# Attention of a hybrid encoder: the order of scores, transposes and products with v in one run for each head pair

## The chip, the cores and the metric

The kernel runs on one core of a Trainium2 chip. The metric is device time in microseconds, from one execution of the whole program. Three runs of the kernel before took 1909.5, 1911.06 and 1911.25 us, a median of 1911.06. One more execution was taken with the hardware profiler, and the rows shown in this document come from it.

The engines are named as in the profile: PE is the matrix engine, PEld its loading of the stationary operand, DVE the vector engine, ACT the scalar engine, POOL the general engine, and SP the engine that issues most transfers.

## The reference

The program computes two layers of an encoder trunk over 512 tokens of 1024 channels, in float32. Each layer has a feed-forward block, a mixer and a second feed-forward block. The mixer is where the change lies:

```python
z = h @ w_in                       # q, k, v, uf, ga, gf
y_na = neighbourhood_attention(q, k, v, rpb) @ w_na_out
y_f = fourier_mix(uf) @ w_f_out
g_na, g_f = sigmoid(ga + gate_bias[0]), sigmoid(gf + gate_bias[1])
return (g_na * y_na + g_f * y_f) @ w_o
```

There are 8 heads of 64 channels. The tokens lie on a grid of 8 rows by 64 columns. A query sees 16 columns of keys around its own. The queries are cut into four blocks of 16 columns (128 queries), and each block reads a band of 32 columns (256 keys), adds a relative position bias and a mask, takes a softmax over the 256 keys and multiplies by v.

## The kernel before

**Numbers.** A float32 operand is split in two: a high part (written by ACT as a rounded copy) and a low part (written by DVE as the difference). A product is three matmuls, high x high, high x low and low x high (`mm3`, lines 292 to 294). Weights arrive as raw tiles and are split into `whi` (line 181) and `wlo` (line 184), two granules ahead of their use, with three buffers each. `split` (lines 298, 299, and 301, 302 with a factor) does the same to activations.

**Attention.** Two heads make a pair `hp` (0 to 3); its channels fill 128 partitions, head e in partitions 64e to 64e+63. A block of work `i` is half a pair: `i = 2 hp + pr`, and it holds two query blocks of both heads. For each block of work there are three parts:

- scores (`att_scores`, line 1123): 12 matmuls with 64 rows of contraction and 256 columns, the two heads in turn, each head in its own half of the rows and with its own bank of PSUM. Behind them comes the softmax: on DVE the sum with the bias and the maximum (line 1133) and the reciprocal (1142), on ACT the exponential (1139) and the scaling (1146). The result `s` is two tiles.
- transposes (`att_trans`, line 1155): 8 transposes of 128x128 into two banks, each then split into a `p` tile by ACT and DVE.
- product with v (`att_out`): 12 matmuls of 256 columns into one bank, whose result is split into the tile `o` of the pair, one head after the other.

`att_step(i)` runs, in this order, the product of block i-2, the transposes of block i-1 and the scores of block i. So a block's softmax has one step to finish. Between two steps stands other work for PE: a projection of q or k for a later pair (`proj_q`, `proj_k`, 24 matmuls of 512 columns in one bank, whose result DVE multiplies by R at line 977 before it is split), or rows of the product of the Fourier branch with its weights (`fill`, eight rows of 12 matmuls, copied by ACT at line 1210). `bias_for(hp)` loads the relative bias of a pair with four transfers on SP and adds the mask with six operations on POOL (line 1106); it has two pairs' worth of buffers.

**Order.** The text of the kernel gives an order. A planner in the build then fixes each engine's own queue: it goes by the order of the text and by when it reckons an operand to be ready, and it can put a later instruction first. Where a block of the text is marked as scheduled by hand, ACT and DVE keep the order of the text. Each engine then runs its queue strictly in order.

**Space.** PSUM is one pool of eight banks (`bank`), shared by all. A pool of 23 slots of 4 KB (`slot`, `hilo`) holds v and its shifted copies (7 tiles), q, k, o, p, the Fourier branch's y, the rows of its product (`fs`), the tiles t1 of the next stage and the raw weights of this stage. A smaller pool of the stage holds `s`, the bias and the mask; `swap_pools(0)` closes it, and with that the loads of the next stage's weights may begin.

Of the kernel before, what the change touches and what calls it, by code (L numbers as in the profile page):

```python
# [92 lines left out]
def encoder_kernel(  # L93
# [15 lines left out]
    def nm(s):  # L109
        uid[0] += 1  # L110
        return f"{s}_{uid[0]}"
# [4 lines left out]
    def hilo(s):  # L116
        t = slot(F32R, s, (2, T))
        return t[:, 0, :], t[:, 1, :]

    def bank(s="ps"):  # L120
        return pp.tile([P, T], F32, tag="ps", name=nm(s))
# [133 lines left out]
    class Stream:  # L255
# [26 lines left out]
        def next(self):  # L282
            self.prep(self.pos + 1 + AHEAD)
            it = self.items[self.pos]
            self.pos += 1
            return it.out
# [4 lines left out]
    def mm3(ps, lh, ll, rh, rl, start, stop, again=False):  # L291
        PE.matmul(ps, lh, rh, start=start, stop=False, skip_group_check=again)  # L292
        PE.matmul(ps, lh, rl, start=False, stop=False, skip_group_check=again)  # L293
        PE.matmul(ps, ll, rh, start=False, stop=stop, skip_group_check=again)  # L294
# [641 lines left out]
    def stage_mixer(l, norm, nxt):  # L936
        mp = mix_pool[0]

        def tmp(dt=F32, s="x"):
            return mp.tile([P, T], dt, tag="tmp", name=nm(s), bufs=8)  # L940
# [29 lines left out]
        def proj_T(scale):  # L970
            ps = bank()
            wh, wl = ws.next()
            for kt in range(DT):
                c = slice(kt * P, (kt + 1) * P)
                mm3(ps, wh[:, c], wl[:, c], *xs[kt], kt == 0, kt == DT - 1)
            t = tmp(s="q")
            V.tensor_tensor(t, ps, R, ALU.mult)
            hi, lo = hilo("q")
            split(hi, lo, t, scale)
            return hi, lo  # L980
# [104 lines left out]
        def proj_q(hp):  # L1085
            q[hp] = proj_T(DH**-0.5)

        def proj_k(hp):
            k[hp] = proj_T(None)
            o.append(hilo("o"))  # L1090

        def bias_for(hp):
            bms[hp] = []
            for e in range(2):
                res = mp.tile([P, 3, 256], F32, tag="bm", name=nm("bm"), bufs=4)
                b = mp.tile([P, BIAS_F], F32, tag="bw", name=nm("bw"), bufs=2)
                base = RPB_N - BIAS_F - ((l * NH + 2 * hp + e) * RPB_H + 7 * RPB_W + 15 - 16 + RPB_PAD)
                for i in range(2):
                    src = bass.AP(tensor=rpb.tensor, offset=base + 8 * i, ap=[[RPB_W, 8], [1, 8], [1, BIAS_F]])
                    nc.sync.dma_start(out=b[64 * i : 64 * i + 64, :], in_=src)  # L1100
                for c in range(3):
                    w = bass.AP(
                        tensor=b.tensor, offset=b.offset + BIAS_F - 1 - OFF[c],
                        ap=[list(b.ap[0]), [-8, 4], [-RPB_W, 8], [-1, 8]],
                    )
                    G.tensor_tensor(
                        res[:, c, :].rearrange("p (a b c) -> p a b c", a=4, b=8), w,
                        msk[:, c, :].rearrange("p (a b c) -> p a b c", a=4, b=8), ALU.add,
                    )
                bms[hp].append(res)  # L1110

        def att_scores(i):
            hp, pr = divmod(i, 2)
            (qh, ql), (kh, kl) = q[hp], k[hp]
            ps = [bank(), bank()]
            for jj in range(2):
                j = 2 * pr + jj
                ks = slice(BAND[j] * 64, BAND[j] * 64 + 256)
                qs = slice(j * P, (j + 1) * P)
                for i, (a, b) in enumerate(((qh, kh), (qh, kl), (ql, kh))):  # L1120
                    for e in range(2):
                        r = slice(64 * e, 64 * e + 64)
                        PE.matmul(
                            ps[e][:, jj * 256 : (jj + 1) * 256], a[r, qs], b[r, ks], start=i == 0, stop=i == 2
                        )
            s_ = [tmp(s="s"), tmp(s="s")]
            nmx = sp.tile([P, 4], F32, tag="nmx", name=nm("nmx"), bufs=4)
            sm = sp.tile([P, 4], F32, tag="sm", name=nm("sm"), bufs=4)
            rs = sp.tile([P, 4], F32, tag="rs", name=nm("rs"), bufs=4)
            for e in range(2):  # L1130
                for jj in range(2):
                    c, z = slice(jj * 256, (jj + 1) * 256), 2 * e + jj
                    V.tensor_tensor_reduce(
                        s_[e][:, c], ps[e][:, c], bms[hp][e][:, pr + jj, :], -1.0, -NEG, ALU.add, ALU.min, nmx[:, z : z + 1]
                    )
            for e in range(2):
                for jj in range(2):
                    c, z = slice(jj * 256, (jj + 1) * 256), 2 * e + jj
                    S.activation(
                        s_[e][:, c], s_[e][:, c], AF.Exp, scale=-1.0, bias=nmx[:, z : z + 1], accum_out=sm[:, z : z + 1]  # L1140
                    )
                V.reciprocal(rs[:, 2 * e : 2 * e + 2], sm[:, 2 * e : 2 * e + 2])
            for e in range(2):
                for jj in range(2):
                    c, z = slice(jj * 256, (jj + 1) * 256), 2 * e + jj
                    S.activation(s_[e][:, c], s_[e][:, c], AF.Copy, scale=rs[:, z : z + 1])
            return s_

        def att_trans(s_):
            res = []  # L1150
            for jj in range(2):
                pt = bank()
                for e in range(2):
                    for c in range(2):
                        PE.transpose(
                            pt[:, (2 * c + e) * P : (2 * c + e + 1) * P],
                            s_[e][:, jj * 256 + c * P : jj * 256 + (c + 1) * P], ident,
                        )
                hi, lo = hilo("p")
                split(hi, lo, pt)  # L1160
                res.append((hi, lo))
            return res

        def att_out(i, p_):
            hp, pr = divmod(i, 2)
            po = bank()
            hs = slice(hp * P, (hp + 1) * P)
            for jj in range(2):
                ph, pl = p_[jj]
                for c in range(2):  # L1170
                    vh, vl = vch[BAND[2 * pr + jj] + 2 * c]
                    cs = slice(c * 256, (c + 1) * 256)
                    mm3(po[:, jj * 256 : jj * 256 + 256], vh[:, hs], vl[:, hs], ph[:, cs], pl[:, cs], c == 0, c == 1)
            pv = po.rearrange("p (a e q) -> p a e q", a=2, e=2)
            oh, ol = [z[:, pr * 256 : pr * 256 + 256].rearrange("p (a q) -> p a q", a=2) for z in o[hp]]
            for e in range(2):
                r = slice(64 * e, 64 * e + 64)
                split(oh[r], ol[r], pv[r, :, e, :])

        sc, pt_ = {}, {}  # L1180

        def att_step(i):
            if 0 <= i - 2 < 8:
                att_out(i - 2, pt_.pop(i - 2))
            if 0 <= i - 1 < 8:
                pt_[i - 1] = att_trans(sc.pop(i - 1))
            if i < 8:
                sc[i] = att_scores(i)


        def rows_of(src, tb, w):
# [11 lines left out]
        def fill(src, to, i, w=None):  # L1203

            w = w or [ws.next(), ws.next()]
            for tb in range(TB):
                if tb % 2 == 0:
                    to[i, tb // 2] = slot(F32, "fs", (2, T))
                ps = rows_of(src, tb, w)
                S.activation(to[i, tb // 2][:, tb % 2, :], ps, AF.Copy)  # L1210
                yield
# [106 lines left out]
        for g in range(4):  # L1318
            four_ch(g)
        proj_q(1)  # L1320
        for hp in range(3):
            bias_for(hp + 1)
            att_step(2 * hp)
            proj_k(hp + 1)
            att_step(2 * hp + 1)
            if hp < 2:
                proj_q(hp + 2)

        def f_rows():
            for i in range(2):  # L1330
                yield from fill(yf, fs, i)


        B = {(i, j): [z[i].bitcast(F32)[:, :, j * 256 : (j + 1) * 256] for z in (hx, lx)] for i in range(2) for j in range(2)}
# [7 lines left out]
            V.tensor_tensor(t[0], t[0], t[1], ALU.add)  # L1342
            yield t

        f_fill = f_rows()
        for i in range(6, 8):
            next(f_fill)
            next(f_fill)
            att_step(i)
        next(f_fill)  # L1350
        next(f_fill)
        first = minus(B[0, 0], B[0, 1], "t1")
        next(first)
        att_step(8)
        swap_pools(0)
        next(f_fill)
        next(first)
        att_step(9)
        t12, _ = next(first)
        ws.prep(ws.pos + 2)  # L1360
        next(f_fill)
        bias = []
        for which in range(2):
            b_ = slot(F32, "gb", (D,))
# [278 lines left out]
```

## Time and profile before

| what | us |
|---|---|
| median of three runs | 1911.06 |
| the profiled execution | 1909.88 |
| its span, first to last instruction | 1908.1 |
| PE busy | 1894.6 (99%) |
| DVE busy | 1609.9 (84%) |
| ACT busy | 1162.8 (61%) |
| PE matmuls | 9189 instructions |
| attention, first score to last transpose, layer 1 | 405.90 to 476.30 |
| attention, first score to last transpose, layer 2 | 1352.30 to 1422.70 |

Times of a row are counted from the start of the span. A row of the timeline gives the start, the duration, the engine, the line, the operation, the tiles written and read, the shape of the array's part and of the operand, and a count of like instructions that followed at once; square brackets hold the idle time of the engine before it and what ended that. Matmuls are pipelined: one of 512 columns shows 0.39 us, but the next starts much earlier. So the pace of PE is read from the starts of rows, not from their durations.

### The profile page before, as it was taken

To read this page: it belongs to the slowest core of one execution; us is meant where nothing else is said; L and a number is where in the kernel's file an instruction comes from. 1 tells how busy PE (TensorE), PEld (TensorE's weight loads), DVE (VectorE), ACT (ScalarE), POOL (GpSimd) and SP (SyncE) were. 2 spreads that over 40 slices of the span, in tenths; PEclk is the share of its full clock that TensorE was granted. 3 is DMA by queue.
4 is the path that set the end of the run, shared out by engine and by line. 5 is a ranking of instruction groups with operands and counts; after the bars stand their busy time and mean duration, and the time that the engine had idled before them with its cause. 6 is when DMAs were issued, how large, how long until landed. Compare 5 with 4: busy or idle time off the path is not lost.

```text
span 1908.1 us, 25170 instructions
## 1 busy us (share of the span) xinstructions
PE 1894.6 (99%) x9189; PEld 1587.4 (83%) x9189; DVE 1609.9 (84%) x2000; ACT 1162.8 (61%) x1676; POOL 199.2 (10%) x246
## 2 busy tenths in 40 slices
PE   9999999999999999999999999999999999999998
PEld 7888888888888888888888888888888888888886
DVE  7877899586989987889997778995769899787898
ACT  6655665457666755566665556663675566555664
POOL 0101010300111010001010100103111101010010
PEclk9999999999999999999999999999999999999999
DMA  9776499321986777649877665974129867766594
GB/s 301 207 208 182 149 255 316 95 73 45 265 214 164 175 195 207 176 152 258 255 188 210 183 177 157 274 267 131 37 95 250 214 169 173 205 180 177 170 279 141
DMA packets 104924, 361.09 MB, mean 189 GB/s; under 512 B 12064, under 2 KB 14240, under 8 KB 104800
## 3 DMA queue, kind: packets, MB, share of 16 engines
q1 hardware_dynamic: 77856, 267.42, 39.9%
q0 software_dynamic: 26800, 92.04, 26.7%
q8 instruction: 72, 1.18, 0.2%
q14 instruction: 52, 0.43, 0.1%
q10 hardware_dynamic: 144, 0.02, 0.0%
HBM read 354.18 MB, written 2.11 MB: 187 GB/s over the span
## 4 chain that ended last, share of the span: by engine, by line
PE 98%; DVE 1%; DMA 1%; ACT 0%; issue 0%; DVEq 0%; ACTq 0%
PE A L453 9%; PE A L454 9%; PE A L456 9%; PE o L453 7%; PE o L454 7%; PE o L456 7%; PE ps L292 5%; PE ps L293 5%; PE ps L294 5%; PE B L453 5%; PE B L454 5%; PE B L456 5%; PE C L454 2%; PE C L453 2%; PE C L456 2%; PE tr L545 2%
## 5 line engine op out<-in xcount | busy, mean ns | idle before, releaser
L181 ACT ACTIVATE whi<-raw 128x1024 fp32r<-128x1024 f32 (+1 forms) x528 | 546.9, 1037 | 428.1 <-PE A L454 127.8
L184 DVE TENSOR_TENSOR wlo<-raw,whi 128x1024 fp32r<-128x1024 f32 (+1 forms) x528 | 629.0, 1196 | 195.7 <-ACT whi L181 194.3
L152 POOL DMA_DIRECT2D raw<-in_wst_dram x158 | 136.0, 870 | 1285.7 <-DMA raw<-in_wst_dram 574.5
L166 DVE TENSOR_TENSOR raw<-raw,raw 128x1024 f32<-128x1024 f32 (+1 forms) x146 | 172.2, 1189 | 1.2
L454 PE MATMUL A<-whi,xl 128*128 128x512 f32 x384 | 149.5, 389 | 0.0
L453 PE MATMUL A<-whi,xh 128*128 128x512 f32 x384 | 149.4, 389 | 0.0
L456 PE MATMUL A<-wlo,xh 128*128 128x512 f32 x384 | 110.5, 389 | 0.0
L176 ACT ACTIVATE whi<-raw 128x1024 fp32r<-128x1024 f32 (+1 forms) x79 | 81.8, 1035 | 41.5 <-PE A L454 12.5
L177 DVE SCALAR_TENSOR_TENSOR wlo<-raw,whi 128x1024 fp32r<-128x1024 f32 (+1 forms) x79 | 93.2, 1192 | 10.9 <-ACT whi L176 10.8
L638 ACT ACTIVATE th<-sn,rh 128x512 f32<-128x512 f32 x80 | 56.9, 714 | 69.0 <-DVE sn L527 69.0
L522 ACT ACTIVATE sn<-A 128x512 f32<-128x512 f32 x96 | 56.4, 589 | 49.4 <-PE A L456 49.4
L456 PEld LDWEIGHTS A<-wlo,xh 128*128 128x128 f32 x384 | 72.1, 188 | 15.0
L454 PEld LDWEIGHTS A<-whi,xl 128*128 128x128 f32 x384 | 72.1, 188 | 14.8
L453 PEld LDWEIGHTS A<-whi,xh 128*128 128x128 f32 x384 | 72.1, 188 | 14.8
L453 PE MATMUL B<-whi,t1h 128*128 128x512 f32 x192 | 76.2, 397 | 0.0
L453 PE MATMUL A<-whi,t3h 128*128 128x512 f32 x192 | 75.3, 392 | 0.0
L453 PE MATMUL C<-whi,xh 128*128 128x512 f32 x192 | 74.9, 390 | 0.0
L453 PE MATMUL A<-whi,t2h 128*128 128x512 f32 x192 | 74.9, 390 | 0.0
L454 PE MATMUL B<-whi,t1l 128*128 128x512 f32 x192 | 74.8, 390 | 0.0
L454 PE MATMUL A<-whi,t3l 128*128 128x512 f32 x192 | 74.8, 390 | 0.0
L454 PE MATMUL C<-whi,xl 128*128 128x512 f32 x192 | 74.7, 389 | 0.0
L454 PE MATMUL A<-whi,t2l 128*128 128x512 f32 x192 | 74.7, 389 | 0.0
(410 smaller groups left out, 4794.3 us busy)
## 6 DMA issues: line engine op xcount, KB each, us to landing
raw<-in_wst_dram SPq DMA_DIRECT2D x466, 512.0 KB
raw<-in_wst_dram POOLq DMA_DIRECT2D x162, 512.0 KB, 7.8
raw<-in_wst_dram SPq DMA_DIRECT2D x30, 256.0 KB
vs<-v SPq DMA_DIRECT2D x12, 256.0 KB
bw<-in_rpb_dram SPq DMA_DIRECT2D x32, 68.0 KB
x<-in_xin_dram SPq DMA_DIRECT2D x4, 512.0 KB
raw<-in_wst_dram POOLq DMA_DIRECT2D x8, 256.0 KB, 8.2
dft<-in_dft_dram POOLq DMA_DIRECT2D x8, 256.0 KB, 6.1
```

Source lines behind the costliest of these rows:

```text
L152: G.dma_start(out=self.t, in_=wst[GRAN_AT[self.plus]][:, 0 : self.n], accum_op=ALU.add)
L166: V.tensor_tensor(self.raw.t, self.raw.t, self.add.t, ALU.add)
L176: S.activation(hi, t, AF.Copy, scale=-1.0)
L177: self.last = V.scalar_tensor_tensor(lo, t, -1.0, hi.bitcast(F32), ALU.mult, ALU.subtract)
L181: S.activation(hi[:, cs], t[:, cs], AF.Copy)
L184: self.last = V.tensor_tensor(lo[:, cs], t[:, cs], hi[:, cs].bitcast(F32), ALU.subtract)
L292: PE.matmul(ps, lh, rh, start=start, stop=False, skip_group_check=again)
L293: PE.matmul(ps, lh, rl, start=False, stop=False, skip_group_check=again)
L294: PE.matmul(ps, ll, rh, start=False, stop=stop, skip_group_check=again)
L453: PE.matmul(ps, lh, rh, start=start, stop=False, skip_group_check=again)
L454: PE.matmul(ps, ll, rh, start=False, stop=False, skip_group_check=again)
L456: PE.matmul(ps, lh, rl, start=False, stop=stop, skip_group_check=again)
```

## The change

`att_scores` is cut in two: the matmuls stay under that name and return their banks, and the softmax becomes `att_probs`. `att_step` is replaced by two functions that work on a whole pair. `att_next(hp)` runs the transposes of both blocks of pair hp-1, then the scores of both blocks of pair hp, and then both softmaxes. `att_outs(hp)` runs the products with v of both blocks of pair hp. The bias of the next pair is now loaded after the scores, and the eight rows of the Fourier product are dealt out as 2, 2, 1, 2 and 1 where they were 2, 2, 2, 1 and 1.

```diff
         def att_scores(i):
...
+            return ps
+
+        def att_probs(i, ps):
+            hp, pr = divmod(i, 2)
             s_ = [tmp(s="s"), tmp(s="s")]
...
-        def att_step(i):
-            if 0 <= i - 2 < 8:
-                att_out(i - 2, pt_.pop(i - 2))
-            if 0 <= i - 1 < 8:
-                pt_[i - 1] = att_trans(sc.pop(i - 1))
-            if i < 8:
-                sc[i] = att_scores(i)
+        def att_outs(hp):
+            for i in (2 * hp, 2 * hp + 1):
+                att_out(i, pt_.pop(i))
+
+        def att_next(hp):
+            if hp:
+                for i in (2 * hp - 2, 2 * hp - 1):
+                    pt_[i] = att_trans(sc.pop(i))
+            if hp < 4:
+                ps = [att_scores(i) for i in (2 * hp, 2 * hp + 1)]
+                for i, p in zip((2 * hp, 2 * hp + 1), ps):
+                    sc[i] = att_probs(i, p)
...
-        for hp in range(3):
-            bias_for(hp + 1)
-            att_step(2 * hp)
-            proj_k(hp + 1)
-            att_step(2 * hp + 1)
-            if hp < 2:
-                proj_q(hp + 2)
+        for hp in range(3):
+            att_next(hp)
+            bias_for(hp + 1)
+            proj_k(hp + 1)
+            if hp:
+                att_outs(hp - 1)
+            if hp < 2:
+                proj_q(hp + 2)
+        f_some(2)
...
-        f_fill = f_rows()
-        for i in range(6, 8):
-            next(f_fill)
-            next(f_fill)
-            att_step(i)
-        next(f_fill)
-        next(f_fill)
+        att_next(3)
+        f_some(2)
+        att_outs(2)
+        f_some(1)
         first = minus(B[0, 0], B[0, 1], "t1")
         next(first)
-        att_step(8)
+        att_next(4)
         swap_pools(0)
-        next(f_fill)
+        f_some(2)
         next(first)
-        att_step(9)
+        att_outs(3)
         t12, _ = next(first)
         ws.prep(ws.pos + 2)
-        next(f_fill)
+        f_some(1)
```

`f_some(n)` takes the next n rows from the generator that `fill` makes.

More of the change, by code (lines that the diff above doesn't have):

```diff
@@ L1331, in f_rows, with f_some @@
                 yield from fill(yf, fs, i)
+        f_fill = f_rows()
+        def f_some(n):
+            for _ in range(n):
+                next(f_fill)
+        for hp in range(3):
[7 more added lines that the diff above has]
+        f_some(2)
         B = {(i, j): [z[i].bitcast(F32)[:, :, j * 256 : (j + 1) * 256] for z in (hx, lx)] for i in range(2) for j in range(2)}
```

## The prediction, made before the changed kernel ran

> **What bounds the kernel now.** I read the page's head first (which engine fills the span), then its chain by engine, then the waits of PE, then the stretches in which the two layers run the changed code.
>
> ```profile
> span 1908.1 us, 25170 instructions
> PE 1894.6 (99%) x9189; PEld 1587.4 (83%) x9189; DVE 1609.9 (84%) x2000; ACT 1162.8 (61%) x1676; POOL 199.2 (10%) x246
> PE 98%; DVE 1%; DMA 1%; ACT 0%; issue 0%; DVEq 0%; ACTq 0%
> ```
> ```profile
> PE ps L138 <- ACT warm L135: 2.7, 1, 2.7
> PE wB L453 <- ACT whi L181: 1.7, 2, 1.0
> ```
> ```profile
> 405.90:476.30 70.40, 70.39 (x439) 59.54 (x438) 45.98 (x129) 54.50 (x144) 8.19 (x12) 1.00 0.11 35
> 1352.30:1422.70 70.40, 70.39 (x439) 59.52 (x438) 45.92 (x129) 54.49 (x144) 8.17 (x12) 1.00 0.11 35
> ```
>
> In the last two (length, then busy time and count of PE, PEld, DVE, ACT, POOL, the granted clock, DMA share and GB/s) the reader sees attention from the first score to the last transpose: PE has no hole, DVE is busy 65% and ACT 77%, the clock is 1.00, DMA is nearly idle. PE waits nowhere in it, so time can be won only from matmuls that PE takes longer over than it must, and these show in their starts. One step of attention, from the timeline of PE; where a row's count falls from x12 to x10, x8 and x2, the same run is read from a later instant, so that its starts can be told apart:
>
> ```profile
> 430.63 0.28 PE L294 MATMUL ps<-p,v 128*128 128x256 f32 x1
> 430.75 1.04 PE L1155 MATMUL ps<-ident,s 128*128 128x128 f32 x8
> 431.51 0.27 PE L1155 MATMUL ps<-ident,s 128*128 128x128 f32 x1
> 431.72 0.97 PE L1123 MATMUL ps<-q,q 64*128 64x256 f32 x12
> 431.94 0.75 PE L1123 MATMUL ps<-q,q 64*128 64x256 f32 x10
> 432.06 0.63 PE L1123 MATMUL ps<-q,q 64*128 64x256 f32 x8
> 432.41 0.28 PE L1123 MATMUL ps<-q,q 64*128 64x256 f32 x2
> 432.62 0.50 PE L292 MATMUL ps<-xh,whi 128*128 128x512 f32 x1
> 432.96 0.40 PE L293 MATMUL ps<-xl,whi 128*128 128x512 f32 x1
> 434.36 0.40 PE L293 MATMUL ps<-xl,whi 128*128 128x512 f32 x1
> 440.63 0.97 PE L1123 MATMUL ps<-q,q 64*128 64x256 f32 x12
> ...
> 483.15 0.39 PE L292 MATMUL ps<-whi,o 128*128 128x512 f32 x1
> 494.03 0.39 PE L453 MATMUL A<-whi,xh 128*128 128x512 f32 x1
> ```
>
> **The price of one run of scores.** Transposes start every 0.109 us (seven in 430.75 to 431.51), but the last one is followed only after 0.21: 0.10 lost. Scores go in pairs, one head of the pair in each half of the rows. Three pairs take 432.06 to 432.41, 0.117 each; the first takes 0.22 (0.10 lost), the last 0.21 (0.09 lost). A full matmul of 512 columns follows the one before after 0.227 us (the 48 of the first product with W_na, 483.15 to 494.03); the first behind the scores takes 432.62 to 432.96, 0.34 (0.11 lost), and the six behind it 1.40 in place of 1.36 (0.04 lost). Together 0.44 us, at every run of scores, eight in a layer. After p·v the transposes begin 0.12 later, the plain pace of 256 columns: merging the products or transposes saves nothing by itself.
>
> The Trainium skill, "TensorEngine Tiling (Array Packing)", Key Properties, says that changing the tiling mode drains TensorE. Read narrowly, it would cover the gaps into and out of the scores alone, 0.19 of the 0.44, and the sum below would be 2.0 in place of 4.0; the rows show all five losses beside a change of tiling and none elsewhere in the step, so I take 0.44.
>
> **The change part by part.**
>
> Scores: eight runs of 12 become four of 24 in each layer. That removes 4 x 2 runs x 0.44 = 3.5 us. No instruction is added or taken away.
>
> Transposes: the first group of a layer waits today, because its cover is one projection (24 x 0.227 = 5.4 us):
>
> ```profile
> 412.74 1.26 PE L1155 MATMUL ps<-ident,s 128*128 128x128 f32 x8
> 413.93 0.39 PE L1123 MATMUL ps<-q,q 64*128 64x256 f32 x2
> 1359.16 1.26 PE L1155 MATMUL ps<-ident,s 128*128 128x128 f32 x8
> 1360.35 0.39 PE L1123 MATMUL ps<-q,q 64*128 64x256 f32 x2
> ```
>
> 1.19 us to the scores against 0.97 above: 0.22 in each layer, 0.4 together. After the change two projections (10.9 us) lie between, so this wait goes, if the softmax of two blocks keeps up. That is the cover to be worked out; the step's work on ACT and DVE:
>
> ```profile
> 430.41 1.04 ACT L181 ACTIVATE whi<-raw 128x1024 fp32r<-128x1024 f32 x1
> 431.36 0.62 ACT L298 ACTIVATE q<-q 128x512 fp32r<-128x512 f32 x1
> 432.28 1.06 ACT L298 ACTIVATE p<-ps 128x512 fp32r<-128x512 f32 x2
> 433.67 0.38 ACT L298 ACTIVATE o<-ps 64x256 fp32r<-64x256 f32 x1 [0.33 <-DVE o L299]
> 435.79 0.51 ACT L1139 ACTIVATE s<-s,nmx 128x256 f32<-128x256 f32 x1 [1.74 <-DVE nmx L1133]
> 437.78 1.69 ACT L1146 ACTIVATE s<-s,rs 128x256 f32<-128x256 f32 x4
> 439.38 1.04 ACT L181 ACTIVATE whi<-raw 128x1024 fp32r<-128x1024 f32 x1
> ```
> ```profile
> 431.49 1.22 DVE L184 TENSOR_TENSOR wlo<-raw,whi 128x1024 fp32r<-128x1024 f32 x1 [1.27 <-ACT whi L181]
> 432.63 0.68 DVE L299 TENSOR_TENSOR q<-q,q 128x512 fp32r<-128x512 f32 x1
> 433.56 0.67 DVE L299 TENSOR_TENSOR p<-ps,p 128x512 fp32r<-128x512 f32 x1
> ...
> 434.73 0.69 DVE L299 TENSOR_TENSOR p<-ps,p 128x512 fp32r<-128x512 f32 x1
> 435.33 0.41 DVE L1133 CUSTOM_DVE_ANT_0 s<-ps,bm 128x256 f32<-128x256 f32 x1
> 436.36 0.42 DVE L1133 CUSTOM_DVE_ANT_0 s<-ps,bm 128x256 f32<-128x256 f32 x1
> ```
>
> The first exponential starts 4.1 us after its scores (431.72 to 435.79); a block then costs ACT 2.0 (435.79 to 437.78) and 1.6 (437.78 to 439.38), two blocks 7.2. PE spends 1.6 on 24 scores, 5.4 on a projection or on two rows of the f product, 1.4 on a block's p·v (12 x 0.12); a block's eight transposes give the second block 0.9 more.
> - First pair: PE 1.6 + 10.9 + 0.9 = 13.4; ACT 4.1 + 7.2 = 11.3, and one weight split and one k split (1.0 + 0.6) if they are queued ahead: 12.9.
> - Second and third: PE 1.6 + 5.4 + 2.9 + 5.4 + 0.9 = 16.2; ACT 11.3 + 1.6, four o splits (4 x 0.4) and, as four p pairs precede and not two, 0.7 x 2 on DVE: 15.9 with everything ahead, 12.7 with nothing.
> - Last: PE 1.6 + 5.4 + 2.9 + 2.7 + 0.9 = 13.5; ACT 11.3, the 1.4, two copies of f rows (0.5 each, as a p half, which has the same 512 columns), a weight split and four o splits: 16.3 with everything ahead, 12.7 with nothing.
> I take 0 for new waits, since what is ready last is seldom queued first; the high end is 16.3 - 13.5 = 2.8 us in each layer, at the last pair. Below nothing there is no room: PE has no other hole here.
>
> Products p·v of a pair: both blocks' p were split more than 5 us before. Nothing. Projection of k: it ends at least 5.4 us ahead of the scores that read it, one weight split and one q split. Nothing.
>
> Moves: the bias work goes behind the scores. POOL's six additions per pair and SP's four loads then have until the next pair's first maximum, about 17 us:
>
> ```profile
> bw<-in_rpb_dram SPq DMA_DIRECT2D x32, 68.0 KB
> ```
> ```profile
> L1106 POOL TENSOR_TENSOR bm<-bw,msk 128x256 f32<-128x256 f32 x12 | 8.2, 724 | 62.7 <-DVE nmx L1133 62.7
> ```
>
> 6 x 0.72 = 4.3 us; no transfer competes (share 0.11). Nothing. The f rows keep their number, and the subtraction for t1 on DVE stays between two PE runs of several us. The loads that the change of pools starts lie 11.0 us ahead of the second product with W_na, not 6.9; PE did not wait there, so nothing is won. Of the 23 slots 23 are taken when the last four p are written (v 7, y 4, o 3, f 3, t1 2, p 4); the fourth o and the last f pair must wait for block 6's product. That holds a copy on ACT back by 1.4 us at most, with a row and the whole W_na product ahead of its reader. Nothing.
>
> **Sum.** -3.5 - 0.4 = about -4.0 us. The profiled execution took 1909.88 us (span 1908.1 and 1.8 around it), so it would take 1905.9; it lies 1.2 under the median of the three runs, 1911.06, which becomes 1907.1. 0.2% is 3.8 us, about what a measurement of this kernel can tell from no change: the forecast is just beyond it.
>
> **Rivals.**
> 1. PSUM fills up (slower). A pair's four transposed banks and four score banks are asked for within 3.2 us, all eight there are; before, a step asked for four. The next projection starts 3.45 us after the first transpose (1.84 + 1.61) and needs the first of them emptied. Today the first low half of p ends 3.5 us after the first transpose (433.56 + 0.67 against 430.75), behind a weight split and a q split: about no wait. If the bank that the planner hands on is the one emptied third, that is 434.73 + 0.69 + 0.6, 5.3 us after the first transpose, and PE waits 1.8 at each of three such bursts a layer: 10.8 us, so 1907.1 + 10.8 = 1917.9. It eats the gain from 0.66 us a burst and is slower by 0.2% from 1.3. For it: the emptying of four score banks takes DVE 8 x 0.35 = 2.8 us. Against it: the p halves come before the maxima in the order of the step, and DVE idles 1.27 us here. The Trainium skill, "TensorEngine Tiling (Array Packing)", Gotcha 1, names this: row tiling raises the pressure on PSUM, since row tiles write different banks. It would speak against every longer run of scores; no run here shows a PE wait on a bank yet.
> 2. Part is lost: the last pair's transposes wait, by half of the 2.8 us a layer: 1907.1 + 2.8 = 1909.9, within 0.2%; by all of it 1912.7.
> 3. It doesn't do what it says: the planner puts a projection's matmuls between two blocks' scores, so that only half the runs merge: 0.4 + 1.8 gained, 1908.9. Against it: in the rows above PE follows the order of the text, p·v, transposes, scores, projection.
> 4. Extra gain: the 1.7 us that PE waits for weights later in the mixer shrink as the later plan shifts: down to 1905.5. Nothing in the rows ties it to attention.
>
> **Chances.** Forecast 0.48, at -4.0 give or take 0.6, so 0.29 beyond -3.8 and 0.19 short of it; rival 4 0.15; rivals 2 and 3 0.21 together; rival 1 0.16, nearly all beyond +0.2% once it sets in. Faster 0.44, same 0.41, slower 0.15. The range 1905.5 to 1912.0 holds the forecast, rivals 3 and 4 and most of rival 2, and leaves rival 1 out; the forecast's own range is 1906.5 to 1907.7.
>
> **What would show it.** Right: four runs of 24 scores in each layer; 17.4 us, not 17.8, from one pair's scores to the next; 0.97 + 0.87 us from the first transpose to the scores in every burst; no new line in PE's waits. Wrong: a PE wait on a bank, with a low half of p or a maximum behind it (rival 1); a gap inside 16 transposes (rival 2); 12-score runs (rival 3).

## The result and the profile after

The changed kernel took 1907.32 us (median of 14 runs, 1906.21 to 1908.28) against 1911.15 us for the kernel before (14 runs beside it): a ratio of 0.9979, with a 95% interval of 0.9971 to 0.9988, or 3.8 us less. A second set of runs, beside experiments 5 and 6, gave 1907.52 against 1909.84, ratio 0.9984 (0.9975 to 0.9993), 2.3 us less by the medians and 3.1 us by the ratio. So the kernel is faster by 0.16 to 0.21%, and the forecast of 1907.1 us lies 0.2 us from the first median. Both intervals exclude no change, but neither shows that the gain is beyond the 0.2% which the prediction set as its mark. The profiled execution took 1906.98 us, 2.90 less than the one before.

The head of the page and the waits of PE, after. The head has the span and the busy time of each engine; a wait has the total in us, how often, and the longest:

```profile
span 1905.2 us, 25187 instructions
PE 1890.9 (99%) x9189; PEld 1586.3 (83%) x9189; DVE 1608.4 (84%) x2000; ACT 1161.3 (61%) x1676; POOL 199.0 (10%) x246
```
```profile
PE wB L453 <- ACT whi L181: 1.6, 2, 1.1
PE ps L292 <- DVE p L299: 0.8, 2, 0.4
```

PE is busy 3.7 us less with the same 9189 matmuls. The last line is new: twice, once in each layer, a projection (line 292) waits for a low half of p.

One burst of the changed kernel, the second in the first layer, from the timeline of PE:

```profile
418.81 1.91 PE L1160 MATMUL ps<-ident,s 128*128 128x128 f32 x16
420.65 1.69 PE L1124 MATMUL ps<-q,q 64*128 64x256 f32 x24
422.72 0.50 PE L292 MATMUL ps<-xh,whi 128*128 128x512 f32 x1 [0.38 <-DVE p L299]
423.06 0.40 PE L293 MATMUL ps<-xl,whi 128*128 128x512 f32 x1
```

Sixteen transposes take 1.84 us to the scores, as forecast (0.97 + 0.87), and 24 scores follow as one run. Behind them stands the wait.

To see what the change is worth apart from the rest of the program, I cut out the stretch that holds all of the moved work: from the first score of a layer to the first matmul that reads `o`. It has the same PE work in both kernels, 472 matmuls (a row counts one or two more, which overlap an end of the stretch). The rows have the ends and the length of the stretch, then the busy time and count of PE, PEld, DVE, ACT and POOL, the clock, the DMA share and GB/s. Before, in both layers:

```profile
406.22:483.15 76.93, 76.92 (x474) 65.37 (x474) 51.64 (x136) 58.36 (x150) 9.96 (x14) 1.00 0.17 58
1352.64:1429.57 76.93, 76.92 (x473) 65.38 (x473) 51.62 (x136) 58.36 (x150) 9.93 (x14) 1.00 0.17 58
```

After:

```profile
406.18:481.58 75.40, 75.01 (x473) 65.00 (x473) 50.59 (x137) 58.19 (x150) 9.94 (x14) 1.00 0.27 78
1351.15:1426.56 75.41, 75.01 (x474) 65.00 (x473) 50.59 (x137) 58.22 (x150) 9.92 (x14) 1.00 0.27 77
```

The two layers of one execution agree to 0.01 us, and a second profiled execution of the changed kernel (experiment 7) has 75.41 and 75.42 us between the same two matmuls, so this view tells far more than a run's time does. The change wins 1.53 and 1.52 us, 3.05 us in all, and PE is idle 0.39 us in each stretch where it was idle 0.01.

### The profile page after: what moved, and what is told of

Same layout as the page of the kernel before. It is cut to its first block, busy times and chain, and to the rows that moved or that the text cites. A ratio compares the mean times of both kernels' runs of the same rounds, so it can differ in the third digit from the quotient of the medians.

```text
span 1905.2 us, 25187 instructions
## 1 busy us (share of the span) xinstructions
PE 1890.9 (99%) x9189; PEld 1586.3 (83%) x9189; DVE 1608.4 (84%) x2000; ACT 1161.3 (61%) x1676; POOL 199.0 (10%) x246
## 4 chain that ended last, share of the span: by engine, by line
PE 95%; DVE 2%; DMA 1%; ACT 1%; issue 0%; SPq 0%; DVEq 0%; ACTq 0%
PE A L453 9%; PE A L454 9%; PE A L456 9%; PE o L454 7%; PE o L453 7%; PE o L456 7%; PE ps L292 5%; PE ps L293 5%; PE ps L294 5%; PE B L453 5%; PE B L454 5%; PE B L456 5%; PE C L454 2%; PE C L453 2%; PE C L456 2%; PE tr L545 2%
## 5 line engine op out<-in xcount | busy, mean ns | idle before, releaser
L184 DVE TENSOR_TENSOR wlo<-raw,whi 128x1024 fp32r<-128x1024 f32 (+1 forms) x528 | 630.1, 1198 | 187.3 <-ACT whi L181 185.2
```

The costliest lines, as they stand in the source:

```text
L184: self.last = V.tensor_tensor(lo[:, cs], t[:, cs], hi[:, cs].bitcast(F32), ALU.subtract)
```

## The experiments

**1. The wait for p: what makes it.** DVE in the burst above, from its timeline:

```profile
418.51 1.22 DVE L184 TENSOR_TENSOR wlo<-raw,whi 128x1024 fp32r<-128x1024 f32 x1 [0.26 <-ACT whi L181]
419.65 0.68 DVE L977 TENSOR_TENSOR q<-ps,R 128x512 f32<-128x512 f32 x1
420.25 1.21 DVE L184 TENSOR_TENSOR wlo<-raw,whi 128x1024 fp32r<-128x1024 f32 x1
421.38 0.68 DVE L302 SCALAR_TENSOR_TENSOR q<-q,q 128x512 fp32r<-128x512 f32 x1
421.99 2.47 DVE L299 TENSOR_TENSOR p<-ps,p 128x512 fp32r<-128x512 f32 x4
```

Two weight splits (L184), a product with R (L977) and the low half of q (L302) stand ahead of the four low halves of p. The first of these ends at about 422.67 (421.99 and 0.68 for one, the length of the like subtraction of q), and PE goes on at 422.72. The experiment takes the low half of q out of the way:

```diff
                 hi, lo = hilo("p")
-                split(hi, lo, pt)
+                with tc.high_priority():
+                    split(hi, lo, pt)
```

> The changed kernel, with the splits of p given high priority, so that DVE writes the low halves of p ahead of the low half of q. Theory (after the second run of scores PE waits 0.4 us a layer for the first transposed bank, which DVE empties behind a low half of q of 0.6 us): the line of PE waiting for DVE p goes, the gap behind those scores falls from about 0.6 to 0.15 us, and the span falls by about 1.0 us against the changed kernel, to about 1904.2; ratio to the kernel before about 0.9975. Rival (the wait is for something else than the order on DVE): the gap stays at 0.6 us and the span at 1905.2.

Measured: 1906.57 us, ratio 0.998 (0.9971 to 0.9989). The same burst on DVE and on PE, and the stretch of both layers:

```profile
421.82 2.48 DVE L299 TENSOR_TENSOR p<-ps,p 128x512 fp32r<-128x512 f32 x4
424.23 0.68 DVE L302 SCALAR_TENSOR_TENSOR q<-q,q 128x512 fp32r<-128x512 f32 x1
```
```profile
419.11 1.91 PE L1160 MATMUL ps<-ident,s 128*128 128x128 f32 x16
420.95 1.69 PE L1124 MATMUL ps<-q,q 64*128 64x256 f32 x24
422.57 0.50 PE L292 MATMUL ps<-xh,whi 128*128 128x512 f32 x1
```
```profile
406.48:481.35 74.87, 74.87 (x474) 65.00 (x473) 50.72 (x137) 58.21 (x150) 9.94 (x14) 1.00 0.28 80
1352.45:1427.34 74.89, 74.89 (x473) 65.00 (x473) 50.71 (x137) 58.20 (x150) 9.93 (x14) 1.00 0.28 79
```

The low half of q now stands behind those of p. From the first transpose to the start of the first low half of p it is 2.71 us where it was 3.18, and from the first transpose to the projection 3.46 where it was 3.91; PE's waits no longer name p. The stretch is 2.06 and 2.04 us shorter than before the change, 4.1 in all, against 3.05 with the wait. So the order on DVE makes the wait. The expected span of 1904.2 did not come in the profiled execution (1905.7), whose time is 0.9 us above the median of this experiment's runs. This kernel's waits lie elsewhere:

```profile
PE wB L453 <- ACT whi L181: 1.4, 1, 1.4
PE A L453 <- ACT sn L522: 0.8, 2, 0.6
```

They stand in the gate blocks (A) and the last product of the mixer (wB); one more, of 0.2 us, stands ahead of the stretch. How much of that the new priorities cause is open: the changed kernel itself, run again, had a span of 1906.1 in place of 1905.2 and other waits there:

```profile
PE wB L453 <- ACT whi L181: 0.9, 2, 0.6
PE ps L292 <- DVE p L299: 0.8, 2, 0.4
PE A L453 <- ACT sn L522: 0.5, 1, 0.5
```

So these two executions of one program differ by 0.9 us outside the stretch, and a gain of 1 us can be shown in the stretch but not in the time. The wait for p alone came back the same, 0.8 us in two times.

**2. Merged scores alone.** Transposes and products with v go block by block, as in the kernel before:

```diff
-            if i < 8:
-                sc[i] = att_scores(i)
+            if i < 8 and i % 2 == 0:
+                ps = [att_scores(j) for j in (i, i + 1)]
+                for j, p in zip((i, i + 1), ps):
+                    sc[j] = att_probs(j, p)
```

> The kernel before, with the scores of a pair's two blocks in one run; transposes and products with v stay block by block as before. Theory (only the number of changes between scores and other matmuls counts): 4 runs less in each of 2 layers at 0.44 us, -3.5 us, and 4 more changes from transposes to a projection a layer at 0.1 us, +0.8: about -2.7 us, 1908.4. Rival (the gain is from merged transposes and products): about 0, 1911.

Measured: 1906.42 us, ratio 0.9979 (0.997 to 0.9987), no wait in attention, and this stretch in each layer:

```profile
406.73:481.68 74.95, 74.95 (x473) 65.08 (x473) 50.65 (x136) 59.07 (x150) 9.91 (x14) 1.00 0.18 61
1350.88:1425.83 74.95, 74.95 (x474) 65.07 (x473) 50.65 (x136) 59.09 (x150) 9.90 (x14) 1.00 0.18 61
```

That is 1.98 us less a layer, 4.0 in all. So the scores' runs (1.76 us, four at 0.44) and the first transposes' wait (0.22 us) make up the whole gain, and what merged transposes and products add is nothing. It is even 1.3 us better than expected. The first part of that is the first transposes' wait, which I had left standing (0.4): here the transposes take 0.79 us to the projection in place of 1.19.

```profile
413.92 1.04 PE L1160 MATMUL ps<-ident,s 128*128 128x128 f32 x8
414.71 0.48 PE L292 MATMUL ps<-xh,whi 128*128 128x512 f32 x1
415.03 0.39 PE L293 MATMUL ps<-xl,whi 128*128 128x512 f32 x1
415.26 0.40 PE L294 MATMUL ps<-xh,wlo 128*128 128x512 f32 x1
```

Most of the rest is that a change from transposes to a projection costs nothing, where I put 0.1 us on each of the eight (0.8). The projection's first matmul starts 0.79 us after the first transpose, where eight at 0.109 would be 0.87, and it is followed after 0.32 in place of 0.23. The two cancel: from the first transpose to the projection's second matmul it is 1.11 us, and the plain paces make 1.10.

**3. Merged transposes and products, scores apart.** The second block's scores go behind the projection of k; for the last pair they go between two rows of the Fourier product (that part of the edit is not shown). `att_one` runs scores and softmax of one block:

```diff
             if hp < 4:
-                ps = [att_scores(i) for i in (2 * hp, 2 * hp + 1)]
-                for i, p in zip((2 * hp, 2 * hp + 1), ps):
-                    sc[i] = att_probs(i, p)
+                att_one(2 * hp)
...
             proj_k(hp + 1)
+            att_one(2 * hp + 1)
```

> The changed kernel, with the two blocks' scores of a pair apart again, a projection or a row of the f product between them; transposes and products with v stay merged. Theory: eight runs of scores a layer again, so all of the gain goes but the 0.4 us of the first transposes' wait: about 1910.7. Rival (transposes and products merged are what gains): about 1908.

Measured: 1910.52 us against 1910.72, ratio 0.9998 (0.9989 to 1.0007). The stretch of the first layer:

```profile
406.68:483.32 76.64, 76.64 (x473) 64.86 (x473) 51.21 (x137) 58.37 (x150) 10.91 (x14) 1.00 0.22 69
```

0.29 us less a layer than before: the gain is gone but for what the first transposes had waited (0.22) and 0.07. With experiment 2 this settles which part of the change counts.

**4. Scores over all 128 rows.** The kernel before, with the heads not separated:

```diff
                     for e in range(2):
-                        r = slice(64 * e, 64 * e + 64)
                         PE.matmul(
-                            ps[e][:, jj * 256 : (jj + 1) * 256], a[r, qs], b[r, ks], start=i == 0, stop=i == 2
+                            ps[e][:, jj * 256 : (jj + 1) * 256], a[:, qs], b[:, ks], start=i == 0, stop=i == 2
```

> The kernel before, with each scores matmul over all 128 rows instead of its head's 64; this leaves the separation of the two heads out of the scores, so both heads get the same sum. Theory (the losses at a run of scores belong to the change between 64-row and 128-row use of the array): all five losses go, the 12 matmuls follow one another every 0.12 us, 1.43 us a run in place of 0.70 + 0.44, so +0.29 x 16 = +4.6 us, about 1915.7, and the first matmul behind the scores is followed after 0.23 us. Rival (the losses belong to the change of operands and of the number of columns): they stay, +0.73 x 16 = +11.6 us, about 1922.7.

Measured: 1914.43 us, ratio 1.0023 (1.0013 to 1.0033). The first run of scores, the second one with the transposes ahead of it, and the stretch:

```profile
406.80 0.39 PE L294 MATMUL ps<-xh,wlo 128*128 128x512 f32 x1
407.03 1.60 PE L1122 MATMUL ps<-q,q 128*128 128x256 f32 x12
408.46 0.40 PE L292 MATMUL ps<-xh,whi 128*128 128x512 f32 x1
408.69 0.40 PE L293 MATMUL ps<-xl,whi 128*128 128x512 f32 x1
```
```profile
413.93 1.03 PE L1154 MATMUL ps<-ident,s 128*128 128x128 f32 x8
414.72 1.68 PE L1122 MATMUL ps<-q,q 128*128 128x256 f32 x12
416.24 0.40 PE L292 MATMUL ps<-xh,whi 128*128 128x512 f32 x1
```
```profile
407.03:486.17 79.14, 79.14 (x474) 70.41 (x472) 51.65 (x136) 59.22 (x151) 9.97 (x14) 1.00 0.17 56
```

All five losses are gone. In the first run it is 0.23 us into the scores, 12 scores take 1.43 us (0.119 each), and 0.23 lies behind the first full matmul. In the second, eight transposes and 12 scores take 2.31 us, and the plain paces make 2.30 (0.87 and 1.43). The same operand tiles and columns with 128 rows cost nothing to enter or to leave. So the losses belong to the 64-row use and the change into and out of it. The edit also ends the two heads' running beside each other; which of the two makes the losses, it does not separate. The stretch is 2.21 us longer, 4.4 for both layers, where 4.6 were expected. The first transposes' wait is gone here (0.79 us to the scores), which makes up 0.4, so a run costs 0.30 more where 0.29 was expected; the 64-row form with its losses is still the cheaper one.

**5. More runs.** The kernel before, with the transposes between two halves of the scores:

```diff
+            if i < 8:
+                att_half(i, ps, (0,))
             if 0 <= i - 1 < 8:
                 pt_[i - 1] = att_trans(sc.pop(i - 1))
             if i < 8:
-                sc[i] = att_scores(i)
+                att_half(i, ps, (1,))
+                sc[i] = att_probs(i, ps)
```

> The kernel before, with the 12 scores of a block in two runs of 6, the eight transposes of the block before between them (the first block has none, so its 12 stay together): 15 runs of scores a layer in place of 8. Theory (each run of scores costs 0.44 us, however long it is): 7 x 2 x 0.44 = +6.2 us, about 1916.9. Rival (the loss goes with the number of scores, or with the matmul behind them, and not with the runs): 0, or 14 x 0.15 = +2.1 us for the matmul behind alone.

Measured: 1914.6 us against 1909.84, ratio 1.0021 (1.0012 to 1.003). One step and the stretch:

```profile
413.31 0.62 PE L1122 MATMUL ps<-q,q 64*128 64x256 f32 x6
413.86 1.10 PE L1157 MATMUL ps<-ident,s 128*128 128x128 f32 x8
414.88 0.62 PE L1122 MATMUL ps<-q,q 64*128 64x256 f32 x6
415.43 0.50 PE L292 MATMUL ps<-xh,whi 128*128 128x512 f32 x1
415.77 0.40 PE L293 MATMUL ps<-xl,whi 128*128 128x512 f32 x1
```
```profile
406.70:485.70 79.00, 79.00 (x473) 65.86 (x473) 51.53 (x136) 59.21 (x150) 9.98 (x14) 1.00 0.18 60
```

+2.07 us a layer for seven more runs. The first transposes' wait of 0.22 is gone here too (1.02 us to the scores in place of 1.19), so the runs cost 2.29, which is 0.33 each and not 0.44. Neither expectation fits. Six scores at 0.117 a pair would be 0.35 us and take 0.55: into, within and out of a run costs the same as before, about 0.30 with the entry. But a run that transposes follow does not pay what a projection pays behind its first matmul (0.34 at 415.43 in place of 0.23); the transposes lose only 0.05 (1.02 us in place of 0.97). So 0.44 is 0.29 for the run and 0.15 for the full matmuls behind it.

**6. Fewer runs.** The changed kernel, with the scores of two pairs at once; `att_four` runs the 48 scores of four blocks and then their softmaxes, `att_tr` the transposes of one pair:

```diff
-        for hp in range(3):
-            att_next(hp)
...
+        proj_k(1)
+        att_four((0, 1))
+        proj_q(2)
+        proj_k(2)
+        att_tr(0)
...
-            return mp.tile([P, T], dt, tag="tmp", name=nm(s), bufs=8)
+            return mp.tile([P, T], dt, tag="tmp", name=nm(s), bufs=9)
```

> The changed kernel taken further: scores of two pairs in one run of 48, two runs a layer; transposes and products with v per pair, apart from the scores. Theory: 6 x 2 x 0.44 = -5.3 us against the kernel before, -0.4 for the first transposes' wait, +0.6 for three more changes from transposes to a projection in each layer: about -5.1 us, 1905.8, if no bank of PSUM is waited for. Rival (eight banks of scores at once make the next projection wait for DVE, which needs 0.7 us to empty one bank): a gap of 0.5 to 2 us behind each of the four runs, -3 to +3 us.

Measured: 1916.72 us, ratio 1.0032 (1.0023 to 1.0041): slower. Its waits of PE:

```profile
PE ps L1124 <- DVE q L299: 3.7, 4, 1.0
PE ps L1160 <- ACT fs L1221: 3.5, 2, 1.8
PE ps L292 <- DVE o L299: 0.6, 2, 0.3
```

7.8 us of waits outweigh the expected 5.1. The places are not the expected ones, behind the runs. The first wait stands inside the run: the second pair's scores follow the projection of their k at once, and its split is not ready. The second stands inside the transposes, until ACT has copied an f row. The first run in the first layer:

```profile
411.48 1.90 PE L1124 MATMUL ps<-q,q 64*128 64x256 f32 x26
414.33 1.58 PE L1124 MATMUL ps<-q,q 64*128 64x256 f32 x22 [0.96 <-DVE q L299]
415.84 0.50 PE L292 MATMUL ps<-xh,whi 128*128 128x512 f32 x1
```

It takes 4.36 us, where 24 pairs at 0.117 and the 0.20 lost in a run make 3.0. So it loses 1.35, of which 0.96 stands as a wait: the stop inside the run costs about 0.4 more. The second run is as long with a wait of 0.88, so by estimate such stops cost 1.7 us more in the four runs. That makes -5.1 + 7.8 + 1.7 = +4.4; the profiled execution took 5.0 us more than the one before and the ratio gives 6.1, so the rest is open. In this order a longer run costs the work that used to cover its operands. Whether a better order of the same two runs would win was not tried.

**7. The changed kernel once more**, as the measure of what executions scatter:

> The changed kernel once more, beside the others: the theory and its rivals all expect 0.998 of the kernel before, and the same two waits for DVE p of 0.4 us.

Measured: 0.9984 (0.9975 to 0.9993); its waits are shown under experiment 1.

No version tried is shown to beat the changed kernel by its time; by the stretch of both layers, experiment 1 is 1.05 us shorter and experiment 2 is 0.9 us shorter.

## Why the prediction was right, point by point

- **The price of a run of scores** (0.44 us, eight to four runs): right for this change, where a projection or f row stands behind every run. Experiment 4 shows that the losses go with the 64-row use, 2 and 3 that the gain goes with the scores' runs alone, 5 that 0.15 of the 0.44 belongs to what stands behind. The Trainium skill, "TensorEngine Tiling (Array Packing)", Key Properties, says that changing the tiling mode drains TensorE. The prediction's narrow reading of that (0.19 us a run from the rows, a sum of 2.0) is refuted by experiment 2's 4.0.
- **The first transposes' wait** (0.4 us): right. Experiment 3 keeps 0.29 a layer of gain with eight runs, and in experiment 2 the first group of transposes takes 0.79 us to what follows, without a wait.
- **"I take 0 for new waits"**: this term was mis-sized; it measured 1.05 us, both layers together. The softmax kept up: in no burst do the 16 transposes wait, so rival 2's place stayed empty. But rival 1's place, the projection behind a burst, cost 0.5 us a layer, at the bank emptied first and not at the third, as rival 1 reckoned: 0.45 at the second burst (3.91 less 3.46 us from the first transpose to the projection) and 0.08 at the third (1.70 us from the first score to the projection, and 1.62 in experiment 1). The step that failed was the estimate that the first low half of p is done 3.5 us after the first transpose; at the second burst it took 3.86. The estimate read the order on DVE from a step before the change, with one weight split and a q split ahead; here two weight splits, a product with R and a q split stand ahead. One of the prediction's signs shows the same: from one pair's scores to the next it is 17.46 us from the third pair to the fourth, close to the forecast 17.4, but 17.83 from the second to the third, with the wait in between.
- **The sum** was -4.0; the stretch gave -3.05, and -4.1 once the wait was gone (experiment 1). The first median's 3.8 comes nearer to the forecast than the stretch supports; the second set's 3.1 by its ratio is what the stretch gives. That agreement of 1907.32 with 1907.1 is thus in part luck of about 0.8 us.
- **Rival 3**: no; all runs hold 24 scores. **Rival 4**: not shown; the wait at the mixer's last product was 1.7 before, 1.6 and 0.9 after.
- **The moves** of the bias, of the f rows, of the change of pools and of the slots cost nothing that the stretch shows: experiment 1, which has them all, leaves PE idle for 0.00 us in it and is 4.1 us shorter.

## What to carry to other kernels

On a PE that never waits, time hides in the starts of the matmuls: compare the gap at each change of shape with the plain pace, and count how often it occurs. Merging the runs wins what each change costs, but it also asks for the banks and operands of two runs at once, so read the order on the emptying engine as it will be after the change, with everything that the longer cover lets in ahead. To show a gain below the scatter of the time, cut out the stretch with the same work and compare its length in every repetition within one execution, and in a second execution too.

## What was not expected of the hardware

A pair of 64-row matmuls of 256 columns takes 0.117 us, two of 128 rows 0.238, so the halves do run beside each other. But one run of 12 gains 0.73 us by it (1.43 less 0.70) and gives 0.44 back at its ends and behind it. By an estimate from these figures a run of six gains next to nothing: 0.37 us, less 0.33 to 0.44.

The first full matmul behind a run of scores is followed 0.11 us late, although it and its follower both use 128 rows; what delays it, these runs do not show. Behind transposes it is followed 0.09 us late as well, but there it has started 0.08 us early (experiment 2), so nothing is lost.
